# Two quads' small state-space products issued as one run of sixteen, into one PSUM bank

## Chip, core and metric

One Trainium2 chip, one NeuronCore of it. The metric is the device time of one execution in microseconds (us), lower is better. The kernel before takes 2794.51 us, the median of three runs (2793.18 to 2795.72).

## What is computed

A trunk of two decoder layers on 256 tokens of width 2048, in float32. Layer 0 mixes tokens by a gated MLP, layer 1 by a state-space layer with complex diagonal states; each is followed by cross-attention to a memory and by a squared-ReLU MLP of width 8192. The change sits in the preparation of the state-space layer, which depends on parameters alone. Cut from the reference:

```python
lam = lax.complex(jnp.minimum(lam_re, LAM_RE_MAX), lam_im)          # 128 groups x 64 states
dt = jnp.exp(log_dt)[:, None]
lam_bar = jnp.exp(lam * dt)
b_bar = ((lam_bar - 1.0) / lam)[..., None] * bmat                   # 128 x 64 x 16
bu = jnp.einsum('gpc,bsgc->sbgp', b_bar, u)                         # u = h @ w_in
_, states = lax.associative_scan(combine, (a, bu), axis=0)          # over 256 positions
y = jnp.einsum('gcp,sbgp->bsgc', cmat, states).real + d_skip * u
```

The kernel cuts the 256 positions into chunks of T = 8. Inside a chunk it needs, for each of the 128 groups, the 16x16 matrices "C times the w-th power of lam_bar times b_bar" for w = 0 to 7, with `d_skip` on the diagonal of the first one. These are the small products.

## The kernel before

**The large matmuls.** Nearly all of the time goes to matrix products of weights with activations. A weight chunk of 128x1024 floats is loaded into `wraw` by a DMA on SyncE's queue (line 123), rounded by ScalarE into `whi` (line 102), and its rest written by VectorE into `wlo` (line 103); TensorE then multiplies in three parts (`whi` by the high and the low part of the activations, `wlo` by the high part). `wraw` has four buffers and a fifth in this MLP; `whi` and `wlo` have three each, so VectorE can be about three chunks ahead of TensorE and no more. In the MLP the up-projection runs in `gemm_feat` (high products line 167, 512 wide; low products line 172, 256 wide; in every second chunk the low ones come first, so that two chunks' low products stand next to each other) and the down-projection in `gemm_hid` (lines 806, 807, 809, all 512 wide).

**The preparation.** `ssm_prep` runs beside the MLP of layer 0, as a list of small steps (`self.side`). Every second weight chunk pops one step, and issues it at a lower priority, so that a scheduler puts its instructions between those of the large matmuls. The groups are handled as 32 quads of four. For a quad q there are three steps:

- `quad(q)`: starts the loads of the factors `lb` and of the next `bcq`, and writes `bb` (lines 1069 to 1071), the stationary side of the small products. There are two `bb` buffers, used in turn.
- `quad_q(q)`: writes `qt` (lines 1079 to 1081, two buffers), stores it to DRAM as `Qd` (line 1088, a DMA on GpSimd's queue, 256 KB), issues the four small products of the quad (line 1092) into a PSUM tile `ps`, evacuates them into `kd` (ScalarE line 1096, VectorE line 1097, on top of a memset by GpSimd, line 1095) and stores `kd` in four DMAs on GpSimd's queue as `Kd` (line 1100).
- `quad_p(q)`: writes `po` (line 1110, then 1112 and 1113, with `tq` from line 1111) and stores it as `Pd` (line 1114, GpSimd's queue). `po` has two buffers, so line 1110 of quad q+2 has to wait until `Pd` of quad q has landed.

A small product multiplies a 128x32 `bb` slice with 128x128 of `qt` in plain float32 and is written to 32 of the 128 PSUM partitions. In the trace each stands as two matmuls, so that a quad's four products are eight. `Pd`, `Qd` and `Kd` are read back at the start of the state-space layer.

A very similar run of small products, with the same sizes and into one bank too, is in that layer: line 1207 (`own`), 32 products in a row, 64 in the trace.

**What sets the order.** Each engine works through its instructions in the order in which the scheduler put them; the same holds for the queues from which GpSimd and SyncE issue DMAs. An instruction that waits holds up all that stands behind it.

Of the kernel before, what the change touches and what calls it, by code (L numbers as in the profile page):

```python
# [9 lines left out]
F32 = mybir.dt.float32  # L10
# [3 lines left out]
ALU = mybir.AluOpType  # L14
AX = mybir.AxisListType

P = 128
# [14 lines left out]
T = 8  # L32
# [6 lines left out]
class Trunk:  # L39
# [861 lines left out]
    def ssm_prep(self, pool):  # L901
# [8 lines left out]
        nc, a = self.nc, self.a  # L910
        v = nc.vector
        W = [P, P]
        NL = 2 * T - 1
# [8 lines left out]
        dsk = pool.tile([P, G // 4], F32, name="dsk", bufs=1)  # L922
        eye = pool.tile([P, 16], F32, name="eye", bufs=1)
# [3 lines left out]
        e = {}  # L927
# [118 lines left out]
        def factors(q, i):  # L1046

            if i == 0:
                e["lb", q] = pool.tile([P, 2, 4, 2, 64], F32, name="lb", bufs=2)
            b = a["b_pc"][q]  # L1050
            src = (bass.AP(tensor=b.tensor, offset=b.offset, ap=[[0, T], [8 * 64, 16], [1, 8 * 64]]),
                   bass.AP(tensor=Ld.tensor, offset=Ld.offset + q * 8 * 64, ap=[[G * 2 * 64, T], [0, 16], [1, 8 * 64]]))
            with self.tc.issue_after(self.fed):
                nc.sync.dma_start(out=e["lb", q][:, i], in_=src[i])
# [19 lines left out]
        def times(out, tmp, n, q, x1, x2):  # L1074
            t1 = T1[:, 0:n, cols(q)].rearrange("p w g -> p g w").unsqueeze(3).broadcast_to([P, 4, n, 16])
            t2 = T2[:, 0:n, cols(q)].rearrange("p w g -> p g w").unsqueeze(3).broadcast_to([P, 4, n, 16])
            b1 = x1.unsqueeze(2).broadcast_to([P, 4, n, 16])
            b2 = x2.unsqueeze(2).broadcast_to([P, 4, n, 16])
            v.tensor_tensor(out=out, in0=t1, in1=b1, op=ALU.mult)
            v.tensor_tensor(out=tmp, in0=t2, in1=b2, op=ALU.mult)  # L1080
            v.tensor_tensor(out=out, in0=out, in1=tmp, op=ALU.subtract)

        def quad_q(q):
            factors(q, 1)
            bcq, bb, tq = e[q]
            qt = pool.tile([P, T + 1, 4, 16], F32, name="qt", bufs=2)
            times(qt.rearrange("p w g c -> p g w c"), tq, T + 1, q, bcq[:, 3], bcq[:, 1])
            nc.gpsimd.dma_start(out=self.Qd[q // 2][q % 2].rearrange("p r n -> r p n"), in_=qt[:, 1:])
            kp = self.ps([P, T, 16])
            for g in range(4):  # L1090
                with self.tc.high_priority(offset=g):
                    nc.tensor.matmul(kp[32 * g:32 * g + 32], bb[:, g], qt[:, 0:T, g, :], start=True, stop=True,
                                     skip_group_check=True)
            kd = pool.tile([P, NL, 16], F32, name="kd", bufs=2)
            nc.gpsimd.memset(kd[:, 0:T - 1, :], 0.0)
            nc.scalar.copy(out=kd[:, T:, :], in_=kp[:, 1:, :])
            v.scalar_tensor_tensor(out=kd[:, T - 1, :], in0=eye, scalar=dsk[:, q:q + 1], in1=kp[:, 0, :],
                                   op0=ALU.mult, op1=ALU.add)
            for t in range(4):
                nc.gpsimd.dma_start(out=self.Kd[q // 2][:, :, q % 2, t], in_=kd[32 * t:32 * t + 16])  # L1100

        def quad_p(q):

# [18 lines left out]
        for q in range(G // 4):  # L1122
            sd += [lambda q=q: quad(q), lambda q=q: quad_q(q)]
            if q == 0:
                sd += [lambda: None] * 2
            sd += [lambda q=q: quad_p(q)]
# [408 lines left out]
```

## Time and profile before

| | |
|---|---|
| median of three runs | 2794.51 us |
| the profiled execution, its own time | 2790.06 us |
| its span (first to last instruction) | 2788.4 us |
| TensorE busy (PE) | 2765.7 us, 99% |
| VectorE busy (DVE) | 1986.2 us, 71% |
| ScalarE busy (ACT) | 1395.3 us, 50% |
| GpSimd busy (POOL) | 236.0 us, 8% |
| granted TensorE clock | 0.999 |
| small products, line 1092 | 256 matmuls in the trace, 779.3 to 1321.5 us |

The small products fall into the stretch from 779 to 1322 us, the MLP of layer 0. In the profile's views a row of the timeline gives the start, the length, the engine, the line, the operation and the tiles written and read; `x8` means that eight such instructions follow each other and are merged into one row. "Idle before" is the time that the engine had nothing to do ahead of an instruction, with the instruction that ended the wait. PE is TensorE's matmuls, PEld its loads of the stationary side.

### The profile page before, as it was taken

The page shows a single profiled execution, that of the slowest core. Times are in us where ns is not written, and L with a number is a line of the kernel's source. Part 1 is how long each engine was busy: PE and PEld are TensorE (multiplying, and loading weights), DVE is VectorE, ACT ScalarE, POOL GpSimd, SP SyncE. Part 2 cuts the span into 40 slices and gives each one's busy share as a digit, 9 for nine tenths or more (in the row PEclk, how much of TensorE's full clock was granted, in tenths as well). Part 3 has the DMA queues.
Part 4 walks back from the last instruction along what each step waited for, and adds up shares of the span by engine and source line. Part 5 has one row for each costly group of instructions (what it writes and reads, how often), then busy time and mean ns, then how long its engine had stood idle before and what let it go on. Part 6 is the DMA issues. An engine that isn't in the chain of part 4 may idle for free. (4 is left out here: it accounts for less than half of the span.)

```text
span 2788.4 us, 39687 instructions
## 1 busy us (share of the span) xinstructions
PE 2765.7 (99%) x15020; PEld 2331.1 (84%) x15020; DVE 1986.2 (71%) x2747; ACT 1395.3 (50%) x1801; POOL 236.0 (8%) x434
## 2 busy tenths in 40 slices
PE   9999999999999999999999999999999999999998
PEld 7888888888888888888887888888888888888886
DVE  6765756778978878787568657557777767677665
ACT  6545545555534444444555445445555545455454
POOL 0100000001022222231213100000000000000000
PEclk9999999999999999999999999999999999999999
DMA  8766655547688888887879767564556566565655
GB/s 294 226 216 216 204 177 179 177 156 250 212 261 258 258 257 259 259 257 224 244 244 266 218 199 238 173 196 159 177 156 219 168 217 198 166 218 171 218 180 156
DMA packets 196048, 593.76 MB, mean 213 GB/s; under 512 B 44960, under 2 KB 47184, under 8 KB 195344
## 3 DMA queue, kind: packets, MB, share of 16 engines
q1 hardware_dynamic: 151968, 532.22, 60.6%
q0 software_dynamic: 43744, 58.95, 7.7%
q8 instruction: 117, 1.92, 0.3%
q14 instruction: 75, 0.61, 0.1%
q10 hardware_dynamic: 144, 0.07, 0.0%
HBM read 567.51 MB, written 23.46 MB: 212 GB/s over the span
## 5 line engine op out<-in xcount | busy, mean ns | idle before, releaser
L103 DVE TENSOR_TENSOR wlo<-wraw,whi 128x1024 fp32r<-128x1024 f32 x892 | 1085.1, 1222 | 490.0 <-ACT whi L102 484.3
L102 ACT CAST whi<-wraw 128x1024 fp32r<-128x1024 f32 x892 | 936.9, 1052 | 853.5 <-PE acc L723 202.8
L167 PE MATMUL acc<-act,whi 128*128 128x512 f32 x3072 | 742.3, 391 | 0.9 <-ACT whi L102 0.9
L167 PEld LDWEIGHTS acc<-act,whi 128*128 128x128 f32 x3072 | 562.8, 188 | 111.7 <-issue 2.6
L172 PEld LDWEIGHTS acc<-act,wlo 128*128 128x128 f32 x3072 | 394.9, 191 | 17.6 <-DVE wlo L103 1.9
L172 PE MATMUL acc<-act,wlo 128*128 128x256 f32 x3072 | 403.6, 283 | 1.4 <-DVE wlo L103 1.0
L152 PE MATMUL acc<-whi,act 128*128 128x512 f32 x1472 | 369.7, 393 | 7.1 <-ACT whi L102 6.3
L152 PEld LDWEIGHTS acc<-whi,act 128*128 128x128 f32 x1472 | 274.9, 189 | 64.9 <-ACT whi L102 6.3
L723 PE MATMUL acc<-whi,act 128*128 128x512 f32 x864 | 232.9, 392 | 0.0
L807 PE MATMUL acc<-whi,hl 128*128 128x512 f32 x544 | 213.3, 392 | 0.0
L806 PE MATMUL acc<-whi,hh 128*128 128x512 f32 x544 | 212.7, 391 | 0.0
L152 PE MATMUL acc<-wlo,act 128*128 128x512 f32 x736 | 197.1, 389 | 0.0
L723 PEld LDWEIGHTS acc<-whi,act 128*128 128x128 f32 x864 | 160.4, 188 | 36.5 <-ACT ends L755 1.9
L152 PEld LDWEIGHTS acc<-wlo,act 128*128 128x128 f32 x736 | 138.2, 188 | 28.9 <-DVE wlo L103 0.2
L723 PE MATMUL acc<-whi,hh 128*128 128x512 f32 x378 | 148.4, 393 | 0.0
L723 PE MATMUL acc<-whi,hl 128*128 128x512 f32 x378 | 147.2, 390 | 0.0
L809 PE MATMUL acc<-wlo,hh 128*128 128x512 f32 x544 | 145.9, 390 | 0.0
L723 PE MATMUL acc<-wlo,act 128*128 128x512 f32 x432 | 133.1, 390 | 0.0
L807 PEld LDWEIGHTS acc<-whi,hl 128*128 128x128 f32 x544 | 102.1, 188 | 23.0 <-issue 2.2
L183 ACT COPY r<-acc 128x512 f32<-128x512 f32 x64 | 37.7, 588 | 166.6 <-PE acc L167 166.6
L809 PEld LDWEIGHTS acc<-wlo,hh 128*128 128x128 f32 x544 | 102.1, 188 | 21.5 <-issue 0.2
L806 PEld LDWEIGHTS acc<-whi,hh 128*128 128x128 f32 x544 | 102.1, 188 | 21.4 <-issue 0.4
(365 smaller groups left out, 2763.7 us busy)
## 6 DMA issues: line engine op xcount, KB each, us to landing
wraw<-in_f_w_up SPq DMA_DIRECT2D x256, 512.0 KB, 4.6
wraw<-in_f_w_down SPq DMA_DIRECT2D x228, 512.0 KB, 4.6
wraw<-in_a_w_in SPq DMA_DIRECT2D x64, 512.0 KB, 4.7
wraw<-in_x_w_q SPq DMA_DIRECT2D x64, 512.0 KB, 3.9
wraw<-in_x_w_k SPq DMA_DIRECT2D x64, 512.0 KB, 4.6
wraw<-in_b_w_out SPq DMA_DIRECT2D x64, 512.0 KB, 4.4
wraw<-in_x_w_v SPq DMA_DIRECT2D x48, 512.0 KB, 3.9
wraw<-in_x_w_o SPq DMA_DIRECT2D x48, 512.0 KB, 4.3
```

The costliest lines, as they stand in the source:

```text
L102: self.nc.scalar.copy(out=hi, in_=src)
L103: return self.nc.vector.tensor_tensor(out=lo, in0=src, in1=hi.bitcast(F32), op=ALU.subtract).ins
L152: nc.tensor.matmul(out[t], a[:, kt, sl], b[:, kk, :], start=st and a is ah, stop=en)
L167: nc.tensor.matmul(acc[:, f, :], hi[:, kk, sl], both[:, kt].rearrange("p a s -> p (a s)"), start=first and kk == 0, stop=last and kk == FK ...
L172: nc.tensor.matmul(acc[:, f, 0:S], lo[:, kk, sl], ah[:, kt, :], start=False, stop=last and kk == FK - 1, skip_group_check=True)
L183: nc.scalar.copy(out=dst, in_=acc[:, :, S:])
L723: mm = lambda s, m, e: nc.tensor.matmul(out, s, m, start=key not in begun, stop=e, skip_group_check=True)
L806: nc.tensor.matmul(acc[:, t, :], ah, hi[:, kk, :], start=kt == 0, stop=False)
L807: nc.tensor.matmul(acc[:, t, :], al, hi[:, kk, :], start=False, stop=False)
L809: nc.tensor.matmul(acc[:, t, :], hid[kt // 4][0][:, kt % 4, sl], lo[:, kk, :], start=False, stop=kt == KT - 1)
```

## The change

The small products of an even quad are put off until those of the odd quad behind it are due; then the eight products of both are issued in a row, into one PSUM tile of twice the width (one bank). `kd` becomes one buffer for both quads instead of two buffers of one, with one memset, one ScalarE copy, two VectorE rows and eight DMAs in a row.

```diff
             nc.gpsimd.dma_start(out=self.Qd[q // 2][q % 2].rearrange("p r n -> r p n"), in_=qt[:, 1:])
-            kp = self.ps([P, T, 16])
-            for g in range(4):
-                with self.tc.high_priority(offset=g):
-                    nc.tensor.matmul(kp[32 * g:32 * g + 32], bb[:, g], qt[:, 0:T, g, :], start=True, stop=True,
-                                     skip_group_check=True)
-            kd = pool.tile([P, NL, 16], F32, name="kd", bufs=2)
-            nc.gpsimd.memset(kd[:, 0:T - 1, :], 0.0)
-            nc.scalar.copy(out=kd[:, T:, :], in_=kp[:, 1:, :])
-            v.scalar_tensor_tensor(out=kd[:, T - 1, :], in0=eye, scalar=dsk[:, q:q + 1], in1=kp[:, 0, :],
-                                   op0=ALU.mult, op1=ALU.add)
-            for t in range(4):
-                nc.gpsimd.dma_start(out=self.Kd[q // 2][:, :, q % 2, t], in_=kd[32 * t:32 * t + 16])
+            e["qt", q] = qt
+            if q % 2:
+                products(q // 2)
+
+        def products(m):
+
+            kp = self.ps([P, 2, T, 16])
+            for i in range(2):
+                bb, qt = e["bb"][i], e.pop(("qt", 2 * m + i))
+                for g in range(4):
+                    with self.tc.high_priority(offset=4 * i + g):
+                        nc.tensor.matmul(kp[32 * g:32 * g + 32, i], bb[:, g], qt[:, 0:T, g, :], start=True, stop=True,
+                                         skip_group_check=True)
+            kd = pool.tile([P, 2, NL, 16], F32, name="kd", bufs=1)
+            nc.gpsimd.memset(kd[:, :, 0:T - 1, :], 0.0)
+            nc.scalar.copy(out=kd[:, :, T:, :], in_=kp[:, :, 1:, :])
+            for i in range(2):
+                q = 2 * m + i
+                v.scalar_tensor_tensor(out=kd[:, i, T - 1, :], in0=eye, scalar=dsk[:, q:q + 1], in1=kp[:, i, 0, :],
+                                       op0=ALU.mult, op1=ALU.add)
+            for i in range(2):
+                for t in range(4):
+                    nc.gpsimd.dma_start(out=self.Kd[m][:, :, i, t], in_=kd[32 * t:32 * t + 16, i])
```

What this does to the order, engine by engine. On TensorE and on ScalarE all that is not a small product or a `kd` copy stands in the same order as before. On VectorE, GpSimd and SyncE the preparation's own rows move. Lines behind the change are 11 lower in the file: 1100 is now the small product, 1107 VectorE's `kd` row, 1111 the store of `Kd`, 1121 to 1125 what was 1110 to 1114.

On TensorE, in the down-projection of the MLP, where the second group of small products stood before (`bb_5745` and `bb_5746` are the two `bb` buffers; a row's `x4` is four products of the program):

```order
L806 MATMUL acc<-whi,hh 128x512
L807 MATMUL acc<-whi,hl 128x512
L806 MATMUL acc<-whi,hh 128x512
L1092 MATMUL ps<-qt,bb_5746 32x128 x4
L807 MATMUL acc<-whi,hl 128x512
```

and now at the same place:

```order
L806 MATMUL acc<-whi,hh 128x512
L1100 MATMUL ps<-qt,bb_5745 32x128 x4
L1100 MATMUL ps<-qt,bb_5746 32x128 x4
L807 MATMUL acc<-whi,hl 128x512
L806 MATMUL acc<-whi,hh 128x512
```

The first group, some 100 rows further up, is gone from there and stands directly ahead of the second. In the whole program there are 16 such places instead of 32; two of the 16 have the 256 wide products of line 172 around them, 14 are followed by 512 wide ones.

On GpSimd's queue before, from the first quads on (the numbered names are the DRAM tensors, each of two quads):

```order
L1100 DMA Kd_5662<-kd 240x1x16 x4
L1088 DMA Qd_5647<-qt 2x64x512
L1044 DMA bcq<-in_b_bc 128x256
L1095 MEMSET kd 128x112
L1114 DMA Pd_5631<-po 128x512
L1100 DMA Kd_5662<-kd 240x1x16 x4
L1044 DMA bcq<-in_b_bc 128x256
L1088 DMA Qd_5647<-qt 2x64x512
L1095 MEMSET kd 128x112
L1114 DMA Pd_5631<-po 128x512
```

and now:

```order
L1111 DMA Kd_5662<-kd 240x1x16 x8
L1088 DMA Qd_5647<-qt 2x64x512
L1125 DMA Pd_5631<-po 128x512
L1044 DMA bcq<-in_b_bc 128x256
L1103 MEMSET kd 128x2x112
L1044 DMA bcq<-in_b_bc 128x256
L1088 DMA Qd_5647<-qt 2x64x512
L1125 DMA Pd_5631<-po 128x512
```

Eight `Kd` stores now stand in a row, and `Qd` and `Pd` of the next two quads stand behind them. Ahead of the first `Pd` are always the eight stores and one `Qd`; in some pairs also a `bcq` load, or the memset.

On VectorE, at the same place of the program, before (po_7311 belongs to quad 3 and po_7456 to quad 4; in brackets are the semaphores that a row waits for, DMASW those of GpSimd's DMAs, DMAHW those of SyncE's; the row of line 1110 that writes po_7456 takes the buffer of po_7166, quad 2):

```order
L1112 TENSOR_TENSOR po_7311<-po_7311,tq_7216 128x4x64 [waits DVE_49]
L103 TENSOR_TENSOR wlo_7386<-wraw_7383,whi_7385 128x1024 [waits DMAHW1_49,PE_49,Activation_49]
L1113 TENSOR_TENSOR po_7311<-po_7311,tq_7216 128x4x64
L1070 TENSOR_TENSOR tq_7358<-F_5686,bcq_7213 128x64 [waits DVE_49]
L658 SCALAR_TENSOR_TENSOR x_5601<-acc_7174,r2_5690,x_5601 128x512 [waits PE_49]
L658 SCALAR_TENSOR_TENSOR x_5601<-acc_7174,r2_5690,x_5601 128x512
L103 TENSOR_TENSOR wlo_7423<-wraw_7420,whi_7422 128x1024 [waits DMAHW3_49,Activation_49]
L103 TENSOR_TENSOR wlo_7441<-wraw_7438,whi_7440 128x1024 [waits DMAHW4_49,PE_49,Activation_49]
L1110 TENSOR_TENSOR po_7456<-lb_7353 128x512 [waits DMAHW2_49,DMAHW0_49,DMASW3_49]
L103 TENSOR_TENSOR wlo_7465<-wraw_7462,whi_7464 128x1024 [waits DMAHW5_49,PE_49,Activation_49]
```

and now (po_7149 belongs to quad 2, po_7435 to quad 4, in the same buffer):

```order
L1123 TENSOR_TENSOR po_7149<-po_7149,tq_7067 128x4x64 [waits DVE_49]
L1124 TENSOR_TENSOR po_7149<-po_7149,tq_7067 128x4x64
L1070 TENSOR_TENSOR tq_7199<-F_5686,bcq_7064 128x64 [waits DVE_49]
L658 SCALAR_TENSOR_TENSOR x_5601<-acc_7157,r2_5690,x_5601 128x512 [waits PE_49]
L658 SCALAR_TENSOR_TENSOR x_5601<-acc_7157,r2_5690,x_5601 128x512
L103 TENSOR_TENSOR wlo_7402<-wraw_7399,whi_7401 128x1024 [waits DMAHW1_49,Activation_49]
L1071 TENSOR_TENSOR bb1_5746<-bb1_5746,tq_7199 128x4x16 [waits DVE_49]
L1080 TENSOR_TENSOR tq_7199<-T2_5685,bcq_7064 128x576 [waits DVE_49]
L103 TENSOR_TENSOR wlo_7420<-wraw_7417,whi_7419 128x1024 [waits DMAHW2_49,PE_49,Activation_49]
L1081 TENSOR_TENSOR qt_7240<-qt_7240,tq_7199 128x4x9x16 [waits DVE_49]
L1121 TENSOR_TENSOR po_7435<-lb_7345 128x512 [waits DMAHW6_49,DMAHW5_49,DMASW6_49]
L103 TENSOR_TENSOR wlo_7444<-wraw_7441,whi_7443 128x1024 [waits DMAHW3_49,PE_49,Activation_49]
```

Before, the last row that writes `po` of quad 2 (line 1113) stands 31 rows ahead of the row that takes its buffer again; now it stands 9 rows ahead, and the store that empties the buffer is issued between the two, behind eight `Kd` and one `Qd`.

For the prediction the large products between a pair of quads and the ones that use certain `wlo` were counted in the new order. "First" is the `wlo` directly behind that line 1121 row, "second" the one after it; a count a+b is a products 512 wide and b 256 wide, from the end of the pair's small products to the first use.

| pair (from 0) | to the first | to the second | VectorE rows from line 1121 to the first, and on to the second |
|---|---|---|---|
| 0 | 89+0 | 101+0 | 1121, 103; then 1122, 1123, 1124, 103 |
| 1 | 64+56 | 64+64 | 1121, 103; then 1123, 1124, 103 |
| 5 | 89+0 | 101+0 | 1121, 103; then 1070, 103 |
| 6 | 73+32 | 73+40 | 1121, 1122, 1123, 103; then 1124, 103 |
| 10 | 92+0 | 104+0 | 1121, 103; then 1122, 1123, 1124, 103 |
| 11 | 89+0 | 89+8 | 1121, 103; then 1070, 103 |

For the eight other pairs among the first 14 the count to the first is 72+64 or more, and for the last two no such row is left.

## Prediction

> **What bounds the kernel now.** I read the page first, for the engine that is busy throughout.
>
> ```profile
> span 2788.4 us, 39687 instructions
> ...
> PE 2765.7 (99%) x15020; PEld 2331.1 (84%) x15020; DVE 1986.2 (71%) x2747; ACT 1395.3 (50%) x1801; POOL 236.0 (8%) x434
> ...
> L103 DVE TENSOR_TENSOR wlo<-wraw,whi 128x1024 fp32r<-128x1024 f32 x892 | 1085.1, 1222 | 490.0 <-ACT whi L102 484.3
> ```
>
> TensorE (PE) has work for 99% of the span. Next I read the busy time by windows in the stretch with the small products, then the waits of each engine from 600 to 1340 us. The window row has the window, then busy us of PE, PEld, VectorE (DVE), ScalarE (ACT) and GpSimd (POOL), the granted clock, the DMA share and GB/s.
>
> ```profile
> 1000.00:1100.00 100.00, 100.00 (x578) 84.42 (x577) 84.65 (x133) 43.39 (x53) 28.95 (x52) 1.00 0.85 256
> ```
>
> The waits (in all, how often, the longest), from the lists of PE, DVE, POOL and of SyncE's queue (SPq):
>
> ```profile
> PE ps L229 <- DVE x L614: 0.5, 1, 0.5
> ...
> DVE wlo L103 <- ACT whi L102: 94.9, 93, 1.9
> ...
> DVE bb L1069 <- PE ps L1092: 17.0, 13, 1.8
> ...
> POOL kd L1095 <- DMA Kd<-kd: 64.0, 28, 4.2
> ...
> SPq L1054 <- DVE po L1112: 11.8, 8, 1.5
> ...
> SPq L123 <- DVE wlo L103: 477.3, 203, 9.9
> ```
>
> In 740 us PE waits 0.5 us. The stretch is therefore bound by what PE is given to do, and everybody else has slack: but DVE's is thin, 85 us of work in 100, and every `wlo` that PE needs passes through DVE's queue in order. A change here can win only by taking PE time away, and can lose by making DVE wait longer than its lead over PE.
>
> **First term: PE time.** The timeline of PE around one group of small products (start, length, line, tiles):
>
> ```profile
> 779.01 0.39 PE L807 MATMUL acc<-whi,hl 128*128 128x512 f32 x1
> 779.33 0.43 PE L1092 MATMUL ps<-qt,bb 128*32 128x128 f32 x8
> 779.68 0.50 PE L806 MATMUL acc<-whi,hh 128*128 128x512 f32 x1
> 780.02 0.39 PE L807 MATMUL acc<-whi,hl 128*128 128x512 f32 x1
> 780.25 1.09 PE L809 MATMUL acc<-wlo,hh 128*128 128x512 f32 x4
> 781.17 0.39 PE L806 MATMUL acc<-whi,hh 128*128 128x512 f32 x1
> ```
>
> and a stretch of PE a little later, which gives the undisturbed steps and a second group:
>
> ```profile
> 845.05 0.42 PE L1092 MATMUL ps<-qt,bb 128*32 128x128 f32 x8
> 845.40 1.22 PE L172 MATMUL acc<-act,wlo 128*128 128x256 f32 x8
> 846.46 3.82 PE L167 MATMUL acc<-act,whi 128*128 128x512 f32 x16
> 850.11 2.08 PE L172 MATMUL acc<-act,wlo 128*128 128x256 f32 x16
> 852.02 3.82 PE L167 MATMUL acc<-act,whi 128*128 128x512 f32 x16
> ```
>
> From start to start a 512 wide product takes (850.11−846.46)/16 = 0.228 us, a 256 wide one (852.02−850.11)/16 = 0.119. From 779.01 to 781.17 stand seven 512 wide products, 7×0.228 = 1.60; the stretch took 2.16. So a group of eight matmuls displaces the stream by 0.56 to 0.57 us, although from its own first start to the next large product are only 0.35: the rest is lost at entering and leaving it. 32 groups cost 32×0.57 = 18.2 us.
>
> What do eight more cost when they stand behind the first eight? The nearest row is the run of the same shape in the state-space layer:
>
> ```profile
> 1427.28 1.95 PE L1207 MATMUL ps<-pq,us 128*32 128x128 f32 x64
> 1429.16 2.11 PE L152 MATMUL acc<-whi,act 128*128 128x512 f32 x8
> ```
>
> From the first small start to the next large product are 1.88 us for 64, against 0.35 for 8: 56 more cost 1.53, or 0.027 each, and eight more 0.22. Bounds: nothing (they overlap entirely with the first eight) and 0.57 (no gain). I take 0.22, since shape, type and bank are the same. The term is 16×(0.57−0.22) = **−5.6 us**; at the bounds −9.1 and 0.
>
> The Trainium skill speaks of such packing ("TensorE: Matmul & The Clock Gate", section "Measured speedup vs the span model"): matmuls in different tiles of the array run together, and one more tile adds about 4 ns. By it eight more would add an estimated 0.03 us and the term would be near −8.6. The 27 ns in the row of line 1207 don't agree with 4 ns.
>
> **Second term: the wait that moves onto DVE's queue.** Line 1121 (1110 before) overwrites `po` of two quads ago, and has to wait until that quad's `Pd` has landed. Before, this had much room: `Pd` was issued here, and the row that needed its buffer ran 23 us later,
>
> ```profile
> 853.26 0.55 POOL L1114 DMA_DIRECT2D Pd<-po  x1 [0.57 <-DVE tq L1070]
> ```
>
> ```profile
> 876.61 0.69 DVE L1110 TENSOR_TENSOR po<-lb 128x512 f32<-128x512 f32 x1
> ```
>
> Now the overwriting row stands 9 rows behind the last write instead of 31, and the first `Pd` behind each pair stands behind eight `Kd` stores and a `Qd` on GpSimd's queue. Those can't be issued before the pair's products are done and evacuated. The time from the pair's end on PE to the landing of this `Pd`, step by step. GpSimd behind the group at 845.05:
>
> ```profile
> 847.24 1.16 POOL L1100 DMA_DIRECT2D Kd<-kd  x2 [8.19 <-issue]
> ...
> 849.90 1.13 POOL L1100 DMA_DIRECT2D Kd<-kd  x2 [1.50 <-issue]
> ```
>
> From the next large product (845.40) to the first `Kd` are 1.84 us (the `kd` rows lie in between). There is a second `kd` row on DVE now. Eight `Kd` issues follow each other every 0.57 (1.13 for two): 4.55. Rows of DVE, by lines (count, then ns min/median/max):
>
> ```profile
> L1097 DVE SCALAR_TENSOR_TENSOR kd<-eye,dsk,ps x32: 219/224/234, 780.7 to 1323.5; 128x16 f32<-128x16 f32 x32
> ...
> L1110 DVE TENSOR_TENSOR po<-lb x32: 679/684/689, 758.2 to 1287.3; 128x512 f32<-128x512 f32 x32
> ...
> L1111 DVE TENSOR_TENSOR tq<-lb x32: 681/688/694, 761.6 to 1287.9; 128x512 f32<-128x512 f32 x32
> ...
> L1112 DVE TENSOR_TENSOR po<-po,tq x32: 416/424/427, 763.9 to 1288.6; 128x256 f32<-128x256 f32 x32
> ...
> L1070 DVE TENSOR_TENSOR tq<-F,bcq x32: 216/225/227, 736.2 to 1276.6; 128x64 f32<-128x64 f32 x32
> ```
>
> The second `kd` row is 0.22. Then `Qd`, whose time from issue to landing stands in the view of tile `qt`:
>
> ```profile
> DMA to landing us min/median/max: 10.1/11.7/14.6
> ```
>
> The one place of before where `Pd` directly follows `Qd`, in GpSimd's timeline, then the landing of that `Qd`, then that of that `Pd`:
>
> ```profile
> 1213.19 0.85 POOL L1088 DMA_DIRECT2D Qd<-qt  x1 [0.32 <-DVE tq L1111]
> 1214.03 0.56 POOL L1114 DMA_DIRECT2D Pd<-po  x1
> ```
>
> ```profile
> DMA to landing us min/median/max: 11.9/11.9/11.9
> ```
>
> ```profile
> DMA to landing us min/median/max: 12.0/12.0/12.0
> ```
>
> `Qd` landed at 1225.1, `Pd` at 1226.0: they share the transfer, and `Pd` ends 0.9 behind. In all 1.84+0.22+4.55+11.7+0.94 = **19.3 us** from the pair's end to the landing.
>
> Against it stands what PE has to do until it needs the `wlo` behind line 1121, by the table of the change, less the DVE rows between (1121 0.69, 1122 0.69, 1123 and 1124 0.42 each, 1070 0.22, line 103 1.22):
>
> - pairs 0 and 5: 89×0.228 = 20.3, less 1.9: 18.4 each
> - pair 10: 92×0.228 = 21.0, less 1.9: 19.1
> - pair 1, second `wlo`: 64×0.228+64×0.119 = 22.2, less 4.0: 18.2
> - pair 6, second: 73×0.228+40×0.119 = 21.4, less 4.7: 16.7
> - pair 11, second: 89×0.228+8×0.119 = 21.2, less 3.4: 17.8
>
> Their sum is 108.6. With 19.3 each `wlo` comes late by 0.9, 0.9, 0.2, 1.1, 2.6 and 1.5 us: 7.2 us in all, at six pairs. The other eight pairs have at least 72×0.228+64×0.119 = 24.0 us of work there: DVE waits, PE does not. `wlo` has three buffers, so DVE can't build up more lead than this. The term is **+7 us**, and the most uncertain one: with `Qd`'s shortest landing (10.1) the 19.3 becomes 17.7, only pair 6 is late, +1.0; with 12.7 it becomes 20.3, +13.2; with its longest (14.6) 22.2, +24.6. Beyond 0.9 each us of landing costs six.
>
> The Trainium skill ("DMA: Bandwidth & Descriptors", "Anatomy of one DMA — SWDGE (gpsimd) path") puts a DMA from GpSimd at about 2.0 us plus its bytes at 436 GB/s, an estimated 2.6 us for 256 KB. By it nothing would be late. The rows above have 11.7.
>
> **What costs nothing.** The copy to `kd` is one instead of two on ACT, which is busy 43 of 100 us. DVE's line 1069 now waits for sixteen matmuls instead of eight before it rewrites `bb`, with line 103 behind it; it waited 1.8 us at most before while PE waited for no `wlo`, and a pair ends 0.22 us later than a group did; I take 0 (if that cover were gone, 16×0.22 = 3.5 us). `kd` has one buffer, so GpSimd's memset waits for the last `Kd` to land, as in 28 of 32 cases before (64.0 us): a pair has twice the time for it. SyncE's loads at line 1054 wait for `po` rows, with weight loads behind them; weight loads wait 477.3 us for free buffers anyway, so a few us there stay hidden.
>
> **The sum.** −5.6+7.2 = +1.6, on the profiled execution's 2790.06 us, which is 4.45 below the median of 2794.51; I lay the difference on the median: **2796 us**. A measurement of this kernel can tell about 0.2%, 5.6 us, from no change.
>
> **The rivals.**
>
> *The cover holds.* `Qd` and `Pd` land faster, or DVE's lead is greater than counted; no `wlo` is late, −5.6: 2788.9 us. For it: a 256 KB `Pd` alone is at a median of 9.6 us in the DMA view. Against it: the one `Pd` directly behind a `Qd` took 12.0.
>
> ```profile
> Pd<-po POOLq DMA_DIRECT2D x32, 256.0 KB, 9.6
> ```
>
> *Products ride free.* The second eight overlap with the first (the rule of 4 ns): 16×0.57 = −9.1, so 2785.4 without a stall, and 2792.6 with the second term as summed. Against it: 64 matmuls of line 1207 take five times as long as eight.
>
> *Stores bunch up, slower.* Eight `Kd`, one or two `Qd` and a `Pd` are in flight together where four `Kd` and one `Qd` were; at a DMA share of 0.85 they land later. It decides from a landing of `Qd` above 12.4: then the late time passes 11.2 us and the net 5.6. With 13.1 (between the median and the longest) it is 7.2+6×1.4 = 15.6 late, +10.0: 2804.5 us, all of it at line 1121. For it: landings up to 14.6 exist. Against it: the median.
>
> That the change doesn't do what it says is no rival: the order has 16 places with sixteen matmuls each.
>
> **The numbers.** Given back (the net within 0.2%): 0.55. Cover holds: 0.18; its price is just at the bound of what can be told, so half of it counts as faster. Products ride free: 0.05, most of it faster. Stores bunch up: 0.22. Faster therefore 0.13, same 0.65, slower 0.22. The range goes from 2788.9 (cover holds) to 2802.5 (a landing of 12.8 us); outside are the free ride and the far end of the bunching.
>
> **What would show it.** In the profile after: sixteen matmuls in a row at line 1100 with 0.57 us from the first to the next large product (0.35+0.22); if 0.4, the products ride free; if 0.7, there is no gain. In DVE's waits, line 1121 waiting for `Pd` behind most pairs, some us each; in PE's waits, lines 172 and 809 waiting for `wlo`, 7 us in about six places. If PE waits under 2 us, the second term is wrong and the time is near 2789; if over 12, the landing was longer than I took, and GpSimd's rows will say by how much. A PE wait on anything else (`whi`, weights) would mean that SyncE's or ACT's order, which I priced at nothing, is what counts.

## The result, and the profile after

The changed kernel takes 2810.15 us (median of 6 runs, 2806.53 to 2821.54), the kernel before beside it 2794.32 us (6 runs, 2792.09 to 2795.72). The ratio is 1.0063, with a 95% interval from 1.0044 to 1.0081: slower by 0.6%, 15.8 us, and outside the range of the prediction (2788.9 to 2802.5).

The profiled execution of the changed kernel has a span of 2811.8 us, 23.4 more than before; it is one of the longer runs of its kernel, and that of before one of the shorter, so the profiles lie farther apart than the medians. First the page, which answers to the first lines shown of before:

```profile
span 2811.8 us, 39580 instructions
...
PE 2771.4 (99%) x15020; PEld 2338.9 (83%) x15020; DVE 1979.8 (70%) x2747; ACT 1393.6 (50%) x1785; POOL 232.3 (8%) x418
```

The number of matmuls is the same, and PE is busy for 6 us more with them, although part of its work became cheaper. The waits of PE from 760 to 1360 us, the stretch of the preparation, where before there were none:

```profile
PE acc L172 <- DVE wlo L103: 10.9, 7, 3.0
PE acc L809 <- DVE wlo L103: 5.9, 3, 2.6
```

and those of VectorE (DVE) in the same stretch, the ones that concern `po`:

```profile
DVE po L1121 <- DMA Pd<-po: 55.4, 10, 8.4
DVE po L1121 <- DMA lb<-Ld: 11.0, 3, 6.2
```

So the wait of which the prediction spoke is there, at the row and for the transfer that it named: ten times, up to 8.4 us, and TensorE then waits for `wlo`, 16.8 us in all instead of 7.2. In the six pairs that the prediction named these waits are 14.6 us; the other 2.1 come at pair 12, where the row was released last by a load of `lb`, 1 us behind `Pd`.

The gain that was to pay for it is there too. PE's timeline around the first pair:

```profile
812.43 0.39 PE L806 MATMUL acc<-whi,hh 128*128 128x512 f32 x1
812.66 0.39 PE L807 MATMUL acc<-whi,hl 128*128 128x512 f32 x1
812.89 0.39 PE L806 MATMUL acc<-whi,hh 128*128 128x512 f32 x1
813.21 0.65 PE L1100 MATMUL ps<-qt,bb 128*32 128x128 f32 x16
813.78 0.50 PE L807 MATMUL acc<-whi,hl 128*128 128x512 f32 x1
814.12 0.40 PE L806 MATMUL acc<-whi,hh 128*128 128x512 f32 x1
814.36 0.40 PE L807 MATMUL acc<-whi,hl 128*128 128x512 f32 x1
```

From the first small matmul to the next large one are 0.57 us for sixteen, where it was 0.35 for eight: the second eight cost 0.22. From 812.43 to 814.36 stand five 512 wide products, 5×0.228 = 1.14 us, and it took 1.93: a pair displaces the stream by 0.79 us, and two groups did so by 1.14. That is about 0.35 for each of 16 pairs, 5.5 us.

Minus 5.5 and plus 16.8 are plus 11.3, and the span grew by 23.4. Where is the rest? The next view has busy time and granted clock in stretches of 3.41 us around one of the waits (window, its length, PE busy, PEld, DVE, ACT, POOL, then the clock, the DMA share and GB/s):

```profile
1222.07:1225.48 3.41, 3.41 (x17) 2.68 (x15) 0.00 (x0) 1.05 (x1) 0.00 (x0) 1.00 0.67 254
1225.48:1228.89 3.41, 0.36 (x3) 0.13 (x2) 2.01 (x4) 0.10 (x1) 0.00 (x0) 1.00 0.45 173
1228.89:1232.30 3.41, 3.41 (x17) 3.41 (x18) 3.41 (x5) 0.94 (x1) 0.00 (x0) 0.50 0.76 249
1232.30:1235.71 3.41, 3.41 (x17) 2.80 (x16) 1.76 (x3) 1.05 (x1) 0.00 (x0) 1.00 0.67 229
```

Behind the gap TensorE runs at half its clock for one whole stretch of 3.41 us. It shows in the matmuls themselves, with the gap in brackets:

```profile
1228.76 3.68 PE L172 MATMUL acc<-act,wlo 128*128 128x256 f32 x16 [3.05 <-DVE wlo L103]
1232.26 2.03 PE L167 MATMUL acc<-act,whi 128*128 128x512 f32 x8
```

The sixteen take 3.50 us from start to start, where before sixteen of the same took 1.91. Five gaps of the profiled execution are followed by such a stretch, 5×3.41/2 = 8.5 us. The mean clock of the run says the same: it is 0.996 after and 0.999 before, and 0.003 of 2811.8 us are 8.4. The last piece is the start: the same row of line 229, far ahead of the preparation, begins at 661.74 us before and at 663.36 after, so 1.6 us of the 23.4 arise ahead of the stretch in question. −5.5+16.8+8.5+1.6 = 21.4 of 23.4.

### The profile page after: what moved, and what is told of

The parts are those of the page before. It is cut to its first block, busy times and chain, and to the rows that moved or that the text cites. A ratio compares the mean times of both kernels' runs of the same rounds, so it can differ in the third digit from the quotient of the medians.

```text
span 2811.8 us, 39580 instructions
## 1 busy us (share of the span) xinstructions
PE 2771.4 (99%) x15020; PEld 2338.9 (83%) x15020; DVE 1979.8 (70%) x2747; ACT 1393.6 (50%) x1785; POOL 232.3 (8%) x418
## 5 line engine op out<-in xcount | busy, mean ns | idle before, releaser
L807 PEld LDWEIGHTS acc<-whi,hl 128*128 128x128 f32 x544 | 102.9, 189 | 22.5 <-issue 1.0
L806 PEld LDWEIGHTS acc<-whi,hh 128*128 128x128 f32 x544 | 102.9, 189 | 21.7 <-issue 0.2
```

Source lines behind the costliest of these rows:

```text
L806: nc.tensor.matmul(acc[:, t, :], ah, hi[:, kk, :], start=kt == 0, stop=False)
L807: nc.tensor.matmul(acc[:, t, :], al, hi[:, kk, :], start=False, stop=False)
```

## The experiments

Each kernel ran beside the kernel before on the same chip; ratios are against that.

**Which wait, and is it the stores?** The first kernel has a third `po` buffer; the room comes from four temporaries of the early preparation, which share it.

```diff
-            po = pool.tile([P, 4, 2, 64], F32, name="po", bufs=2)
+            po = pool.tile([P, 4, 2, 64], F32, name="po", tag="po", bufs=3)
```

> The changed kernel with a third po buffer (room for it comes from four temporaries of the early preparation, which now share its space), so that line 1121 (1122 here) overwrites the po of three quads ago. Theory A (the whole loss is this row's wait for Pd, which leaves VectorE late with wlo, and the halved TensorE clock behind each long gap; the gain on TensorE is there): waits of po for Pd near 0, TensorE idle in the stretch under 1 us, no halved clock before the end, and 16 x 0.35 = 5.5 us below the kernel before: 2788.9 us (2787 to 2791). Theory B (the bunched stores and reordered loads disturb the DMA queues, whoever waits): still above 2800. Theory C (grouping itself costs TensorE more than its row shows): above 2795 with no waits.

Measured: 2792.58 us against 2793.58, ratio 0.9995 [0.9986, 1.0004]. The waits for `Pd` are gone, and with them 17 us of the loss; but 2788.9 was not reached. PE's waits from 760 to 1360 us, then DVE's:

```profile
PE acc L172 <- DVE wlo L103: 3.8, 3, 2.9
```

```profile
DVE bcq L1063 <- DMA bcq<-in_b_bc: 19.6, 6, 5.5
DVE po L1122 <- DMA lb<-Ld: 16.1, 8, 5.7
```

Two other loads of the same preparation are now late in the place of `Pd`, one of them by 5.7 us, with a gap on PE of 2.9 us and a halved stretch behind it. So the wait for `Pd` was the largest of several: everything that serves the preparation is short of time. That spoke against the stores as the only cause.

The control, the kernel before with the same third buffer:

> Control: the kernel before with the same third po buffer. Every theory: no change, 2794.3 us (2792 to 2796), since line 1110 did not wait for Pd there. If it is faster, the buffer by itself is worth something and has to be taken off the gain of the first kernel.

Measured: 2792.94, ratio 0.9997 [0.9988, 1.0006]. The buffer by itself is worth nothing.

The third kernel issues the eight `Kd` stores behind the next even quad's `Pd`:

```diff
-            for i in range(2):
-                for t in range(4):
-                    nc.gpsimd.dma_start(out=self.Kd[m][:, :, i, t], in_=kd[32 * t:32 * t + 16, i])
+            e["kd"] = m, kd
...
-            nc.gpsimd.dma_start(out=self.Pd[q // 2][:, q % 2], in_=po.rearrange("p t r s -> p t (r s)"))
+            ins = nc.gpsimd.dma_start(out=self.Pd[q // 2][:, q % 2], in_=po.rearrange("p t r s -> p t (r s)")).ins
+            if "kd" in e and (q % 2 == 0 or q == G // 4 - 1):
+                m, kd = e.pop("kd")
+                with self.tc.issue_after(ins):
+                    for i in range(2):
+                        for t in range(4):
+                            nc.gpsimd.dma_start(out=self.Kd[m][:, :, i, t], in_=kd[32 * t:32 * t + 16, i])
```

> The changed kernel with two po buffers, but the eight Kd stores of a pair are issued behind the Pd of the next even quad. GpSimd's queue then has Qd, Pd, Kd x8 where it had Kd x8, Qd, Pd, so this Pd no longer waits for the pair's products. Theory A: the time from the last po row to the landing falls to about 14 us, the long waits of line 1121 go, and the time is 2789 to 2792 us. Theory B: the stores are bunched as before, eight in a row, so still above 2800.

Measured: 2806.93, ratio 1.0040 [1.0027, 1.0053]. Theory A had this wrong. Theory B had the time (above 2800), but the first kernel, 2792.58 us with the stores bunched, speaks against it. VectorE still waits for `Pd` ten times, 36.1 us in all where it was 55.4. The timelines tell why; first GpSimd (POOL), then DVE:

```profile
1206.34 0.56 POOL L1123 DMA_DIRECT2D Pd<-po  x1 [1.76 <-DVE tq L1070]
1206.91 3.42 POOL L1129 DMA_DIRECT2D Kd<-kd  x6
```

```profile
1210.93 0.42 DVE L1121 TENSOR_TENSOR po<-po,tq 128x256 f32<-128x256 f32 x1
1211.27 0.42 DVE L1122 TENSOR_TENSOR po<-po,tq 128x256 f32<-128x256 f32 x1
1216.72 0.69 DVE L1119 TENSOR_TENSOR po<-lb 128x512 f32<-128x512 f32 x1 [5.03 <-DMA Pd<-po]
```

`Pd` is issued at once when its rows are written, ahead of the stores, and lands 10.3 us later. But DVE stands at the row that wants the buffer after 5.3 us: it has finished the second quad's rows too, and has nothing else to put between. (The stores now stand ahead of the odd quad's `Pd`: that of quad 25 is issued 6.9 us behind its last row, and VectorE waits 3.0 us until it has landed. PE has no wait behind that one.) The changed kernel shows the same. GpSimd there, at pair 11 (its products end at 1205.21), with the landing of this `Pd` in the view of its tile:

```profile
1207.03 4.52 POOL L1111 DMA_DIRECT2D Kd<-kd  x8 [14.51 <-DVE bb L1069]
1211.48 0.88 POOL L1088 DMA_DIRECT2D Qd<-qt  x1
1212.87 0.58 POOL L1125 DMA_DIRECT2D Pd<-po  x1 [0.51 <-DVE tq L1070]
```

```profile
DMA to landing us min/median/max: 14.0/14.0/14.0
```

The stores are out by 1211.5, and `Pd` waits for the DVE rows and not for them, if only by 0.5 us. DVE's rows of both quads stand within 13 us behind the pair; the timeline has the last `po` row of the first at 1212.16, that of the second at 1218.04, and then the wait:

```profile
1212.16 0.42 DVE L1124 TENSOR_TENSOR po<-po,tq 128x256 f32<-128x256 f32 x1
...
1218.04 0.42 DVE L1124 TENSOR_TENSOR po<-po,tq 128x256 f32<-128x256 f32 x1
1226.88 0.69 DVE L1121 TENSOR_TENSOR po<-lb 128x512 f32<-128x512 f32 x1 [8.42 <-DMA Pd<-po]
```

From this comes theory D: the pair holds both `bb` and both `qt` buffers until its products are done, so that the next two quads can't be prepared until then, and are prepared in one burst behind it. No load or store has time enough in a burst.

The fourth kernel doubles a suspected cost: four of the eight stores are issued twice.

> The changed kernel with four of the eight Kd stores of each pair issued twice: four more issues, 4 x 0.57 = 2.3 us, ahead of Qd and Pd. Theory A: each of the seven late pairs is later by 2.3 us, 16 us more idle time, other pairs become late too, and more gaps halve the clock (1.7 us each): 2828 to 2850 us. Theory C: no more than 2 us slower than the changed kernel, 2810 to 2813.

Measured: 2832.65, ratio 1.0140 [1.0126, 1.0154], 22.5 us above the changed kernel. DVE's wait for `Pd`:

```profile
DVE po L1121 <- DMA Pd<-po: 93.0, 14, 11.5
```

Inside the burst each us of stores costs its full price and more, as theory A and the prediction said; theory C, with 2813 at most, is out. Here `Pd` does stand behind the stores: at pair 11 its rows are done 7.4 us behind the pair's end, as in the changed kernel, but it is issued after 13.7 us instead of 7.7. Theories A and D both allow this; it shows the price, not the cause.

**Without the burst.** Four `bb` and three `qt`; the temporaries of the early preparation are placed in the room of `tq`, `po` and `qt`. `po` keeps two buffers, and the stores stay eight in a row.

```diff
-            e["bb"] = [pool.tile([P, 4, 2, 16], F32, name=f"bb{i}") for i in range(2)]
+            e["bb"] = [pool.tile([P, 4, 2, 16], F32, name=f"bb{i}") for i in range(4)]
...
-            bb = e["bb"][q % 2]
+            bb = e["bb"][q % 4]
...
-            qt = pool.tile([P, T + 1, 4, 16], F32, name="qt", bufs=2)
+            qt = pool.tile([P, T + 1, 4, 16], F32, name="qt", tag="qt", bufs=3)
...
-                bb, qt = e["bb"][i], e.pop(("qt", 2 * m + i))
+                bb, qt = e["bb"][(2 * m + i) % 4], e.pop(("qt", 2 * m + i))
```

> The changed kernel with four bb and three qt buffers instead of two and two (room from the temporaries of the early preparation), two po buffers as before and the eight Kd stores still bunched. The next quad's rows no longer have to wait for the pair's products, and on VectorE the row that overwrites po stands 25 to 42 rows behind the last write of that buffer, where the changed kernel has 8 to 30 and the kernel before 22 to 37. Theory D (the loss comes from the preparation being pressed into bursts of two quads, because the pair holds both bb and both qt until its products are done): no waits of po for Pd, no TensorE gap over 1 us in the stretch, no halved clock there, and 5.5 us below the kernel before: 2788 us (2786 to 2790.5). Theory A (the eight stores ahead of Pd are the cause): the stores stand where they stood, so most of the loss stays, above 2800.

Measured: 2786.87 against 2792.64, ratio 0.9978 [0.9969, 0.9987]: 5.8 us faster than the kernel before, where theory D had 5.5. The list of PE's waits from 760 to 1360 us is empty, and the clock of the run is 0.999. What DVE waits for in that stretch has no `po`, no `lb` and no `bcq`:

```profile
DVE wlo L103 <- ACT whi L102: 88.6, 87, 2.5
DVE r L184 <- ACT r L183: 13.6, 19, 2.1
DVE qt L1081 <- PE ps L1102: 7.4, 7, 1.2
DVE x L658 <- PE acc L809: 5.9, 5, 2.1
DVE wlo L103 <- PE ps L1102: 1.2, 1, 1.2
```

And GpSimd at the same pair, with the landing of its `Pd`:

```profile
1188.16 3.96 POOL L1113 DMA_DIRECT2D Kd<-kd  x7
1192.29 0.57 POOL L1113 DMA_DIRECT2D Kd<-kd  x1 [0.17 <-DMA Kd<-kd]
1192.84 0.82 POOL L1090 DMA_DIRECT2D Qd<-qt  x1
1193.65 0.59 POOL L1127 DMA_DIRECT2D Pd<-po  x1
```

```profile
DMA to landing us min/median/max: 13.3/13.3/13.3
```

The eight stores stand in a row ahead of `Qd` and `Pd`, and this `Pd` takes 13.3 us. It lands at 1207.0, and the row that wants the buffer runs at 1214.71 without a wait: the rows are spread again.

But this `Pd` is that of quad 25. With more buffers `Qd` and `Pd` of quad 24, as of each even quad, are issued ahead of the eight stores, in an order of `Kd`, `Qd` and `Pd` that the kernel with the stores later has too. So the stores did not stand where they stood, as the expectation says, and against the changed kernel alone this run does not part the buffers from the order. The kernel with the stores later does: in the same order, with two `bb` and two `qt`, it took 2806.93. Quad 24 shows what the buffers change. From its last `po` row until VectorE is at the row that overwrites the buffer are 21.7 us before, 5.9 in the changed kernel and 30.0 here; its `Pd` took 9.6, 14.0 and 14.1 us to land. Here it is issued and lands so:

```profile
1168.56 0.55 POOL L1127 DMA_DIRECT2D Pd<-po  x1 [2.03 <-DVE po L1126]
```

```profile
DMA to landing us min/median/max: 14.1/14.1/14.1
```

With a third `po` buffer besides:

> As the first kernel, with a third po buffer besides. Theory D: nothing more to gain, within 1 us of the first, 2788 us. If the first still waits for Pd somewhere, this one doesn't.

Measured: 2788.35, ratio 0.9982 [0.9973, 0.9990]; that is 1.5 us above the kernel with two `po` buffers, where within 1 was expected, but the intervals overlap. The kernel before with all these buffers:

> Control: the kernel before (products quad by quad) with the buffers of the second kernel. All theories: as the kernel before, 2793.6 us (2792 to 2795); what it gains has to be taken off the gain of the others.

Measured: 2793.63, ratio 1.0001 [0.9992, 1.0010]: the whole gain is that of the products in pairs. With a fourth `qt` buffer:

> As the first kernel with a fourth qt buffer and two po buffers: po's rows stand 31 to 45 behind, even a little farther than with three. Theory D: 2788 us, within 1 us of the first.

Measured: 2787.02, ratio 0.9979 [0.9970, 0.9988], as with three.

**Which buffer, and the stores once more.** Four `bb` with two `qt`:

> Four bb buffers but two qt, with products in pairs. The rows that overwrite po stand 10 to 30 behind the last write (changed kernel 8 to 30, with four bb and three qt 25 to 42). Theory D (bursts, because the pair holds the buffers): most short distances are still there, so the waits for Pd stay at about the same places, somewhat shorter: 2797 to 2810 us. If one of the two buffers alone were the cause, this or the next kernel would be at 2787.

Measured: 2830.24, ratio 1.0121 [1.0100, 1.0142]. That one buffer alone doesn't help was right, the size was not: it is 20 us worse than the changed kernel. Its waits, of PE and of DVE:

```profile
PE acc L172 <- DVE wlo L103: 17.9, 7, 5.6
PE acc L809 <- DVE wlo L103: 8.0, 3, 4.0
```

```profile
DVE po L1123 <- DMA Pd<-po: 60.3, 9, 9.6
...
DVE bb L1071 <- DMA bcq<-in_b_bc: 9.3, 1, 9.3
```

The rows that overwrite `po` wait about as much in all, but each wait is longer, a load of `bcq` has become late (the gap of 5.6 us on PE is behind it), and the clock of the run is 0.992. So theory D has no account of this run's size; why the waits are longer there was not tried. Three `qt` with two `bb`:

> Three qt buffers but two bb, with products in pairs. Distances 8 to 28. Theory D: as the changed kernel, 2804 to 2815 us.

Measured: 2801.16, ratio 1.0032 [1.0019, 1.0046], still slower than before and 3 us under the range expected. Both buffers are needed.

The kernel that took 2787, with twelve stores:

> Four bb and three qt buffers (the kernel that took 2787), with four of the eight Kd stores of each pair issued twice, so that 2.3 us more of issues stand ahead of the stores behind them on GpSimd's queue. Theory D: the distances of 25 to 42 rows cover it, no wait of po, 2786 to 2789 us. Theory A (the stores themselves are the cost, 2.3 us at each pair): 16 us or more above 2787, at least 2800.

Measured: 2789.34, ratio 0.9986 [0.9976, 0.9995], 2.5 us above the kernel without the extra stores, with intervals that overlap, and its PE waits 0.9 us in the stretch; no row of `po` waits. Four stores more cost 22.5 us where the rows are pressed into bursts and 2.5, hardly clear of noise, where they are not. The control for the room:

> Control: the changed kernel with its own buffer counts, and only the temporaries of the early preparation placed in the room of tq, po and qt, as in the other three. All theories: as the changed kernel, 2804 to 2815 us; if it were near 2790, the room and not the buffers would be what helped.

Measured: 2810.46, ratio 1.0060 [1.0041, 1.0079], as the changed kernel.

**The sum over the runs.** For each: the waits of PE for `wlo` in the stretch, the clock of the run, its difference to before's 0.999, times the span, the two with −5.5, and the difference of the medians that was measured.

| kernel | PE waits | clock | lost by clock | sum | measured |
|---|---|---|---|---|---|
| changed kernel | 16.8 | 0.996 | 8.4 | +19.7 | +15.8 |
| third `po` | 3.8 | 0.998 | 2.8 | +1.1 | −1.0 |
| stores later | 11.2 | 0.996 | 8.4 | +14.1 | +13.4 |
| twelve stores | 29.7 | 0.992 | 19.8 | +44.0 | +39.1 |
| four `bb`, three `qt` | 0 | 0.999 | 0 | −5.5 | −5.8 |
| the same, twelve stores | 0.9 | 0.999 | 0 | −4.6 | −3.4 |
| four `bb`, two `qt` | 25.9 | 0.992 | 19.8 | +40.2 | +37.5 |
| two `bb`, three `qt` | 10.2 | 0.997 | 5.6 | +10.3 | +8.4 |
| control for the room | 17.5 | 0.995 | 11.3 | +23.3 | +17.7 |

The clock has three places, so that column is good to 1.4 us; and in three kernels (stores later, four `bb` with two `qt`, two `bb` with three `qt`) it holds a halved stretch of 1.7 us outside the preparation, between 1521 and 1554 us. The waits and the clock are those of one profiled execution, the measured column is of medians. The three terms give the order of all nine kernels, to 6 us, and the sign of all but the third `po`, which can't be told from no change.

## Why the prediction was wrong

Two steps failed: the size of the second term (7.2 us of waits on PE, measured 16.8), and the price of such a wait, which the sum took at its own length (the halved clock behind it took 8.5 us more).

- **The first term was right.** 0.35 us per pair, 5.5 in all, forecast 5.6; the kernel with the buffers has it whole. The second eight products neither rode free nor cost their full price. Here the trace of before had the very shape in question, at line 1207.
- **The place of the second term was right.** `po`, `Pd`, `wlo`, and TensorE behind them; the six pairs that were named are all late, and one more, pair 12.
- **Its size was not.** "In all 1.84+0.22+4.55+11.7+0.94 = 19.3 us": in the six pairs it was 19.6 to 22.4, on average 21.1. `Qd` landed after 11.7 to 14.2 us there, 12.9 on average, and I had taken the median of the trace of before, 11.7. Of the 1.8 us that are missing 1.2 lie there, and 0.5 in `Pd`, which landed on average 1.4 behind `Qd` and not 0.94. Against the sum of 108.6 that makes 6×21.1−108.6 = 18 us late, and the PE waits at these six pairs are 14.6. Pair 12, whose 2.1 us make up the rest, had been counted as covered. The prediction says itself that each us of landing costs six; so steep a term needs the upper half of its range as its centre when the change itself crowds the transfers.
- **A term was missing.** The sum "−5.6+7.2 = +1.6" takes a wait of TensorE at its own length. Each long gap costs another 1.7 us, since the clock is halved for the next 3.41 us: 8.5 us here. Even with the true waits the sum would have been −5.6+16.8 = +11.2; the halved clock makes it +19.7, on the profiled execution.
- **The chain was read from one end.** I made `Pd` late because "the first `Pd` behind each pair stands behind eight `Kd` stores and a `Qd`". In the trace after, `Pd` waits for its own rows in four of the six pairs; they are done 7.4 us behind the pair's end, just when the queue is through the stores and `Qd`, and in pairs 1 and 10 `Pd` stands behind `Qd` for another 1.6 and 0.7 us. So two chains end at about the same time, and it is partly luck that the sum over the one came near. The stores' move alone left 13.4 us of the 15.8, and in the same order of the stores the buffers took all of it away. The order listing had the cause in it: rows 9 apart instead of 31 say that two quads' work is pressed together, whatever is stored between them.
- **Of the rivals** the slower one, 2804.5 us, came nearest: it has the late time nearly right (15.6 against 16.8) at the row that it named, though it too leaves out the halved clock. But its cause, transfers that bunch up, is not the root: with the bursts gone the `Pd` of quad 24 takes 14.1 us, as long as with them, and nobody waits. It had 0.22.
- **The edits priced at nothing**: line 1069 waits 3.9 us in the stretch where it was 17.0, and `kd`'s single buffer 13.7 us where it was 64.0; both cost nothing. The `lb` loads of line 1054 did not stay hidden: DVE waits 11.0 us for them, and in the kernel with a third `po` buffer they are, with `bcq`, what comes next.

## What to carry to other kernels

When small work is gathered into larger groups, its inputs are held until the whole group is done; with as many buffers as the group has members, the engine that prepares them can only work in bursts, and every load and store of the preparation is then short of time at once. Count the buffers first: here the gathering was worth 5.8 us with two more `bb` and one more `qt` than the pair holds (three of each was not tried), and cost 15.8 without. Where TensorE is the bound, price a wait at more than its length.

## What was not expected of the chip

TensorE's clock is granted in stretches of 3.41 us that lie on a fixed raster: the halved ones of the changed kernel begin at 836.35, 877.31, 1051.39, 1191.34 and 1228.89 us, which are 12, 51, 41 and 11 such stretches apart. What decides is how long TensorE was busy in the stretch before. The windows of the raster, in pairs of one with a gap and the next:

```profile
832.94:836.35 3.41, 1.35 (x6) 0.77 (x5) 1.34 (x2) 0.43 (x1) 0.00 (x0) 1.00 0.24 96
836.35:839.76 3.41, 2.87 (x7) 2.29 (x8) 3.38 (x8) 1.04 (x1) 0.55 (x1) 0.50 0.53 153
873.90:877.31 3.41, 1.55 (x10) 1.35 (x11) 3.41 (x8) 1.05 (x1) 0.56 (x1) 1.00 0.35 82
877.31:880.72 3.41, 3.41 (x13) 2.94 (x12) 3.38 (x4) 0.62 (x1) 0.00 (x0) 0.50 0.83 293
1010.43:1013.84 3.41, 2.79 (x13) 1.97 (x11) 1.55 (x2) 1.05 (x1) 0.00 (x0) 1.00 0.78 239
1013.84:1017.25 3.41, 3.08 (x14) 2.55 (x14) 3.41 (x7) 1.05 (x1) 0.00 (x0) 1.00 0.71 243
```

and one more, from the same kernel:

```profile
1263.02:1266.43 3.41, 1.72 (x8) 1.10 (x6) 2.30 (x3) 1.48 (x2) 0.00 (x0) 1.00 0.25 95
1266.43:1269.85 3.42, 2.98 (x20) 2.65 (x21) 3.38 (x8) 1.05 (x1) 0.55 (x1) 1.00 0.77 137
```

Busy for 1.35 or 1.55 of 3.41 us, the next stretch is halved; busy for 2.79 or 1.72, it is not. Half of 3.41 is 1.71, so in these runs a stretch that is idle for more than about half of its time halves the next one. Over all the traces, for stretches at full clock, the change lies between 1.63 and 1.80 us idle, with both outcomes in between. A gap of 1.87 us that lies across two stretches (the last pair of rows, 1.69 us of it in the first) costs only its length, one of 2.1 us inside a single stretch costs 1.7 us more. A stretch that is itself halved needs far less: in the kernel with four `bb` and two `qt` the one from 1281.04 us was busy for 2.77 of 3.41 us and the next was halved again; with twelve stores the one from 1242.70 was busy for 2.82, and the next was not.

The Trainium skill has this raster ("TensorE: Matmul & The Clock Gate", section "What's actually happening": a free-running window of 3413 ns), and the traces agree with it. The advice of the Trainium skill on the same page to avoid idle gaps of over about 3 us (section "Why this matters for your kernels") is too lenient for this kernel: the gaps ahead of the five halved stretches are 2.1 to 3.1 us long, and only one of them is over 3.
